# Three first column tiles on half 0, four modulation dots on VectorE, and down units of 1024 columns

## The chip, the cores and the metric

One core of a Trainium2 chip runs the whole computation as one program. The metric is device microseconds per execution. TensorE multiplies (in the profile PE, and PEld for its weight loads), VectorE (DVE), ScalarE (ACT) and GpSimd (POOL) work on tiles in SBUF or PSUM, SyncE (SP) issues the transfers. Each engine runs its own instructions strictly in the order in which they were written; semaphores make one wait for another.

## The reference, cut to what matters

Two layers work on 1024 tokens of width 1024 (a context of 256 tokens feeds only the first mixer). Layer 0 mixes with a recurrent block (RG-LRU), layer 1 with a Conformer convolution; each is followed by a gated FFN with a 3x3 depthwise convolution between its two products.

```
for i in range(DEPTH):                                   # 2
    mod = s_c @ ada_w[i] + ada_b[i]                      # 6 x 1024 modulation values
    sh1, sc1, g1, sh2, sc2, g2 = split(mod, 6)
    h = h + g1 * mixer(rmsnorm(h, norm_mix[i]) * (1 + sc1) + sh1)
    xm2 = rmsnorm(h, norm_ffn[i]) * (1 + sc2) + sh2
    u = dwconv2d(xm2 @ w_up, cw, cb, rows, width)        # 1024 -> 5632 channels, 3x3 on a 16 x 64 grid
    v, g = jnp.split(u, 2, axis=-1)
    h = h + g2 * ((silu(g) * v) @ w_down)                # 2816 -> 1024
return rmsnorm(h, norm_final)

def conformer_conv(xm, ...):
    a, g = split(xm @ w1 + b1, 2)                        # 1024 -> 2 x 1024
    v = dwconv1d(a * sigmoid(g), cw, cb)                 # 31 taps
    return silu(layernorm(v)) @ w2 + b2
```

## The kernel before

All tensors lie channels on partitions, tokens along the free dimension, so a column tile is 128 output channels by 1024 tokens. Every fp32 operand is split into a high and a low part, and a product is three matmuls (high x high, high x low, low x high). A column tile has 8 k steps of 6 matmuls, two for each of the three products, one per half of the tokens: 48 matmuls of 512 columns. PSUM is four tiles P[0] to P[3], each of two banks of 512 columns (half 0 and half 1).

**An FFN** (`ffn`, lines 1050 to 1179) runs over 22 pairs p of a value tile and a gate tile. I number the 44 column tiles t0 to t43 as they come: t2p is the value tile of pair p, t2p+1 its gate. A tile's conv (`ffn_conv`) is one ScalarE instruction that starts the accumulator `cv` from PSUM and eight VectorE instructions that add the other taps from PSUM. Then follow a SiLU on ScalarE, the product on VectorE (`cv<-cv,cv`), and the split of z into zh (ScalarE) and zl (GpSimd). The tile's PSUM place is free again when its conv is over.

The place is chosen by a counter `nt`: t0 and t1 on P[0] and P[1] (`first_pair`), each later tile on `nt % 3`, so t42 is on P[0] and t43 on P[1]. P[3] belongs to the down product: from pair 3 on, `between` issues, after every second k step of a column tile, one unit of 6 matmuls that multiplies two z tiles into one bank of P[3], the banks taking turns, and VectorE adds it to the residual h (`h<-ps,mod,h`, 512 columns). The last four z tiles go through `k_outer(4, ..., (2, 3, 0, 1))`, line 1179: it accumulates eight output tiles at a time, two in each PSUM tile, going to P[2], P[3], P[0] for its first three k, and to P[1] only with the fourth. The last gate tile's conv runs in two halves of tokens (`last_gate`).

**The start of a stage.** An RMS norm of the residual needs the sum of squares of all eight tiles (`nacc`); `norm_half` sends it through a product with a constant matrix (the stat, `ps<-nacc,ones`), a ScalarE square root and a VectorE reciprocal (`rs`), and applies it to eight tiles (`xmh`, `xml`). Half 0 is normalised while the stage before still ends; `first_pair` (line 513) then runs t0 on half 0, the stat of half 1, t1 on half 0, and both tiles on half 1. It is used at the start of both FFNs and of the Conformer.

**The modulation** of layer 1, and the last part of layer 0's, is computed during the first FFN as 56 dots of one row of `ada_w` with the vector `sC`: the row is loaded into one of two `raw` buffers, GpSimd multiplies, ScalarE sums. The `raw` buffers also take the down weights. 24 earlier dots (for layer 0's mixer) run as one VectorE instruction each.

**Order.** The kernel simulates itself while it is built (`Order`, lines 65 to 164): each operation has an assumed duration, an engine and a priority; TensorE's program is taken in the order written, and after each piece the operations of the other engines that could have started by then are emitted, the earliest start first, then the lower `prio`, then the one written first. So the written order of TensorE's work, and the assumed times, set where an instruction stands in each engine's queue. On the chip nothing overtakes.

Of the kernel before, what the change touches and what calls it, by code (L numbers as in the profile page):

```python
# [21 lines left out]
ND = D // P  # L22
# [258 lines left out]
class Net:  # L281
# [228 lines left out]
        self.act(512, hi, t, AF.Identity, [tB] + ABs, [hB], bias=B)  # L510
        self.stt(512, lo, t, B, hi.bitcast(F32), ADD, SUB, [tB, hB] + ABs, [lB])

    def first_pair(self):

        slots = [self.w_next() for _ in range(2)]
        x = lambda h, k: [(self.xmh[h][:, k, :], self.xml[h][:, k, :])]
        step = lambda i, h, k: self.k_step(
            slots[i], k, [self.P[i][:, h, :]], x(h, k), k == 0, k == ND - 1, list(self.xB[h][k]), [self.PB[i][h]])
        for i in range(2):
            for k in range(ND):  # L520
                step(i, 0, k)
            if i == 0:
                self.norm_half(*self.pending)
        for k in range(ND):
            for i in range(2):
                step(i, 1, k)

    def ada_dot(self, l, q, eng="dve", after=()):  # L530

        t, b = self.load_raw(self.a["ada"][l, q], after=after)
        col, mB = self.mod[l][:, q:q + 1], self.modB[l][q // 8]
        if eng == "dve":
            self.stt(1024, t, t, 1.0, self.sC, MULT, MULT, [b, self.sCB], [b], [mB], accum=col, after=after)
        else:
            self.tten(1024, t, t, self.sC, MULT, [b, self.sCB], [b], eng=eng)
            self.act(1024, t, t, AF.Copy, [b], [b], [mB], accum=col)

    def ada_bias(self, l, part):  # L540
        m = self.mod[l][:, part * 8:part * 8 + 8]
        b = self.modB[l][part]
        self.tten(8, m, m, self.v("ada_b", l * 48 + part * 8, 8), ADD, [b, self.vB], [b])

    def ada_scale(self, n, l, part, norm):

# [503 lines left out]
    def ffn(self, l, end, last=None):  # L1050
        o = self.o
        g2 = self.modcol(l, 5)
        dn, zr, cv = Ring(self.dn), Ring(self.zt), Ring(self.cv)
        Z, nb = {}, [0]

        def load_down(g, c0, cols, slot):

            t, b = self.raw.next()
            n = 2 * cols
            src = self.a["down"][l, 2 * g:2 * g + 2, :, c0:c0 + cols].rearrange("t p c -> p t c")  # L1060
            self.dma(t[:, :n].rearrange("p (t c) -> p t c", t=2), src, P * n * 4, w=[b])
            hi, lo, hB, lB = slot
            self.split(t[:, :n], b, (hi[:, :n], lo[:, :n], hB, lB), n=n)
            v = lambda x: x[:, :n].rearrange("p (t c) -> p t c", t=2)
            return v(hi), v(lo), hB, lB, c0

        def unit(g, d, hf, w):
            hi, lo, hB, lB, c0 = w
            b = nb[0] % 2
            nb[0] += 1  # L1070
            out, outB = self.P[3][:, b, :], self.PB[3][b]
            c, x = slice(d * P - c0, d * P + P - c0), slice(hf * 512, hf * 512 + 512)
            seq, r = [], [hB, lB]
            for i in range(2):
                zh, zl, zB = Z[2 * g + i]
                r += zB[hf]
                seq += [(hi[:, i, c], zh[:, x]), (hi[:, i, c], zl[:, x]), (lo[:, i, c], zh[:, x])]

            def go():
                for i, (w_, y) in enumerate(seq):  # L1080
                    self.mm(out, w_, y, i == 0, i == 5)

            o.pe(6 * self.mm_us, go, r, [outB])
            h, hB_ = self.h[:, d, x], self.hB[d][hf]
            self.stt(512, h, out, g2(d), h, MULT, ADD, [outB, hB_, self.modB[l][5]], [hB_], prio=-1)


        todo = []
        state = {"q": None, "n": 0, "step": 0}
        quarters = {}  # L1090

        def quarter(g, q):
            quarters[g, q] = load_down(g, q * 256, 256, dn.next())

        def between():
            state["step"] += 1
            if state["step"] % 2 == 0 and todo:
                g, q, d, hf = todo.pop(0)
                unit(g, d, hf, quarters[g, q])
                if (d, hf) == (2 * q + 1, 1):  # L1100
                    del quarters[g, q]
                    nxt = (g, q + 3) if q < 1 else (g + 1, q - 1)
                    if nxt[0] < NF // 2 - 2:
                        quarter(*nxt)

        def zsplit(p, a, aB):
            zh, zl, zhB, zlB = zr.next()
            Z[p] = zh, zl, [[zhB, zlB]] * 2
            self.act(1024, zh, a, AF.Copy, [aB], [zhB])
            self.tten(1024, zl, a, zh.bitcast(F32), SUB, [aB, zhB], [zlB], eng="pool")  # L1110

        def last_gate(f, pt, a, aB, acc, accB):

            zh, zl, zhB, zlB = zr.next()
            Z[NF - 1] = zh, zl, [[Buf(after=[b]) for b in (zhB, zlB)] for _ in range(2)]
            for h in range(2):
                b, c = Buf(after=[aB, accB]), slice(h * 512, h * 512 + 512)
                (hB, lB), av, gv = Z[NF - 1][2][h], a[:, c], acc[:, c]
                self.ffn_conv(l, f, pt, acc, b, h * 8, h * 8 + 8, -2)
                self.act(512, gv, gv, AF.Silu, [b], [b])  # L1120
                self.tten(512, av, av, gv, MULT, [b], [b], prio=-3)
                self.act(512, zh[:, c], av, AF.Copy, [b], [hB])
                self.tten(512, zl[:, c], av, zh[:, c].bitcast(F32), SUB, [b, hB], [lB], prio=-3)

        nt = 0
        ada = [(0, q) for q in range(40, 48)] + [(1, q) for q in range(48)] if l == 0 else []
        if ada:
            self.modB[0][5].begin()
            for p in range(6):
                self.modB[1][p].begin()  # L1130
        for q in range(3):
            quarter(0, q)
        for p in range(NF):
            if p >= 3 and p % 2 == 1 and p < NF - 1:
                g = (p - 3) // 2
                todo += [(g, q, d, hf) for q in range(4) for d in (2 * q, 2 * q + 1) for hf in range(2)]
            pts, accs = [], []
            if p == 0:
                self.first_pair()
                pts, nt = [0, 1], 2  # L1140
            for i, f in enumerate((p, NF + p)):
                if p:
                    self.col_tile(self.w_next(), nt % 3, between)
                    pts.append(nt % 3)
                    nt += 1
                acc, accB = cv.next()
                accs.append((acc, accB))
                if f < 2 * NF - 1:
                    self.ffn_conv(l, f, pts[i], acc, accB)
            (a, aB), (gt, gB) = accs  # L1150
            if p < NF - 1:
                self.act(1024, gt, gt, AF.Silu, [gB], [gB])
                self.tten(1024, a, a, gt, MULT, [aB, gB], [aB])
                zsplit(p, a, aB)
            else:
                last_gate(2 * NF - 1, pts[1], a, aB, gt, gB)
            for _ in range(4 if p < 3 else 3):
                if ada and p >= 1:
                    self.ada_dot(*ada.pop(0), "pool")
            if l == 0 and p == 2:  # L1160
                self.ada_bias(0, 5)

        if l == 0:
            for p in range(6):
                self.ada_bias(1, p)
            self.ada_scale(2, 1, 1, "norm_mix")
            self.ada_scale(3, 1, 4, "norm_ffn")
            m = self.mod[1][:, 16:24]
# [24 lines left out]
    def conformer(self, pool):  # L1193
# [31 lines left out]
        def summed(m):  # L1225

            for h in range(2):
# [2 lines left out]
                if m == 0:  # L1230
                    self.act(512, la, c, AF.Copy, [cvB[m][h]], [lB_])
                elif m not in LATE:
                    self.tten(512, la, la, c, ADD, [lB_, cvB[m][h]], [lB_], eng="pool")

        def taps(m, pt):

# [60 lines left out]

        for m in range(ND):
            if m == 0:
                self.first_pair()  # L1300
                sigmoid(m, 0)
            else:
                self.col_tile(self.w_next(), 0)
                sigmoid(m, 0)
                self.col_tile(self.w_next(), 1)
            glu(m, 1)
            hm = self.h[:, m, :]
# [126 lines left out]
```

## Time and profile before

| | us |
|---|---|
| median of 3 runs | 2446.95 (2445.36 to 2448.15) |
| the profiled execution | 2447.42 |
| its span, first to last instruction | 2445.6 |
| TensorE busy | 2336.1 (96%), 10440 matmuls |
| VectorE busy | 1915.0 (78%) |
| ScalarE busy | 966.6 (40%) |
| GpSimd busy | 808.0 (33%) |
| mean granted TensorE clock | 0.980 |

Busy shares are means over stages of different character. The granted clock is the share of TensorE's full speed in a stretch; 1.00 is 2.4 GHz and 0.50 is 1.2 GHz. In a timeline, the bracket at the end of a row gives how long the engine had been idle just before and which instruction's end released it. Equal instructions in a row are put together (x2, x17), with the time of all.

### The profile page before, as it was taken

Reading aid. Unit: us, or ns where it says so; the run is one execution under the profiler, and the core shown is the slowest. Engines: PE = TensorE matmul, PEld = TensorE weight load, DVE = VectorE, ACT = ScalarE, POOL = GpSimd, SP = SyncE. Lnnn points to the kernel's source line nnn. Section 1 sums busy time; section 2 is a strip of 40 time slices with the busy share of each in tenths; the row PEclk is TensorE's granted clock in tenths of the full one; section 3 lists DMA queues with packets and bytes.
Section 4 is the critical chain, followed back from the end, with each engine's and each line's share of the span. In section 5 each row is a group of like instructions: output and inputs, shape, how many; then the busy total and the mean of one; then the engine's idle time right before and its main releaser. Section 6 shows DMA issues by size and latency. Waiting matters only on the chain. (4 is left out here: it accounts for less than half of the span.)

```text
span 2445.6 us, 26204 instructions
## 1 busy us (share of the span) xinstructions
PE 2336.1 (96%) x10440; PEld 1893.9 (77%) x10440; DVE 1915.0 (78%) x1888; ACT 966.6 (40%) x1145; POOL 808.0 (33%) x413
## 2 busy tenths in 40 slices
PE   7999999889899999999998999699999999999997
PEld 2788788677688888888886888577788888888886
DVE  7677878776878778777888888677888777777877
ACT  5578778544433333333225332365322221222223
POOL 1100000355545554544423243245323322332323
PEclk9999999899999999999999999899999999999998
DMA  7324325352222323222111242422111111111101
GB/s 268 113 81 147 94 78 169 103 195 99 93 97 96 103 86 104 95 90 101 65 44 35 74 126 85 138 69 91 52 48 52 32 51 52 52 51 49 44 26 70
DMA packets 82443, 214.99 MB, mean 88 GB/s; under 512 B 8528, under 2 KB 33104, under 8 KB 82192
## 3 DMA queue, kind: packets, MB, share of 16 engines
q1 hardware_dynamic: 80448, 210.68, 26.4%
q10 hardware_dynamic: 1872, 2.62, 0.3%
q8 instruction: 82, 1.34, 0.2%
q14 instruction: 41, 0.34, 0.0%
HBM read 192.10 MB, written 13.63 MB: 84 GB/s over the span
## 5 line engine op out<-in xcount | busy, mean ns | idle before, releaser
L361 DVE SCALAR_TENSOR_TENSOR cv<-ps,vec,cv 128x960 f32<-128x960 f32 (+2 forms) x720 | 860.7, 1197 | 143.7 <-ACT cv L353 128.1
L440 PE MATMUL ps<-xmh,whi 128*128 128x512 f32 x2272 | 747.0, 396 | 19.3 <-ACT xmh L353 12.3
L440 PE MATMUL ps<-xmh,wlo 128*128 128x512 f32 x2272 | 739.9, 393 | 6.9 <-POOL wlo L368 5.2
L440 PE MATMUL ps<-xml,whi 128*128 128x512 f32 x2272 | 740.5, 393 | 4.2 <-DVE xml L361 4.1
L368 POOL TENSOR_TENSOR wlo<-wraw,whi 128x1024 fp32r<-128x1024 f32 (+1 forms) x164 | 397.8, 2440 | 703.0 <-ACT whi L353 689.4
L440 PEld LDWEIGHTS ps<-xmh,whi 128*128 128x128 f32 x2272 | 429.3, 190 | 117.7 <-ACT xmh L353 15.9
L440 PEld LDWEIGHTS ps<-xml,whi 128*128 128x128 f32 x2272 | 430.7, 190 | 102.9 <-DVE xml L361 8.4
L440 PEld LDWEIGHTS ps<-xmh,wlo 128*128 128x128 f32 x2272 | 430.2, 189 | 101.0 <-POOL wlo L368 7.8
L361 DVE SCALAR_TENSOR_TENSOR h<-ps,mod,h 128x512 f32<-128x512 f32 (+1 forms) x360 | 262.6, 733 | 161.6 <-PE ps L440 161.5
L353 ACT ACTIVATE cv<-ps,vec 128x1024 f32<-128x1024 f32 (+1 forms) x90 | 105.9, 1181 | 364.0 <-PE ps L440 352.9
L353 ACT ACTIVATE whi<-wraw 128x1024 fp32r<-128x1024 f32 (+1 forms) x198 | 202.2, 1042 | 111.0 <-DMA wraw<-w_out_in 34.1
L368 POOL TENSOR_TENSOR zl<-cv,zh 128x1024 fp32r<-128x1024 f32 x42 | 101.4, 2415 | 416.1 <-ACT zh L353 416.1
L440 PE MATMUL ps<-zh,dnh 128*128 128x512 f32 x576 | 227.8, 395 | 6.3 <-DVE h L361 5.9
L440 PE MATMUL ps<-zl,dnh 128*128 128x512 f32 x576 | 224.8, 390 | 5.0 <-POOL zl L368 5.0
L440 PE MATMUL ps<-zh,dnl 128*128 128x512 f32 x576 | 227.0, 394 | 0.0
L368 POOL TENSOR_TENSOR raw<-raw,sC 128x1024 f32<-128x1024 f32 x56 | 134.9, 2412 | 141.5 <-DMA raw<-ada_in 141.5
L353 ACT ACTIVATE cv<-cv 128x1024 f32<-128x1024 f32 (+1 forms) x46 | 47.1, 1023 | 309.3 <-DVE cv L361 301.0
L361 DVE SCALAR_TENSOR_TENSOR CV<-ps,vec,CV 128x1009 f32<-128x1009 f32 (+14 forms) x120 | 153.0, 1275 | 8.7 <-ACT CV L353 5.1
L368 POOL TENSOR_TENSOR dnl<-raw,dnh 128x512 fp32r<-128x512 f32 x72 | 93.5, 1299 | 176.6 <-ACT dnh L353 176.5
L353 ACT ACTIVATE raw<-raw 128x1024 f32<-128x1024 f32 x56 | 59.2, 1057 | 231.2 <-POOL raw L368 231.2
L440 PEld LDWEIGHTS ps<-zl,dnh 128*128 128x128 f32 x576 | 108.7, 189 | 31.2 <-POOL zl L368 5.8
L440 PEld LDWEIGHTS ps<-zh,dnh 128*128 128x128 f32 x576 | 108.4, 188 | 29.3 <-DVE h L361 6.4
(140 smaller groups left out, 2420.9 us busy)
## 6 DMA issues: line engine op xcount, KB each, us to landing
raw<-ada_in SPq DMA_DIRECT2D x88, 512.0 KB, 3.6
wraw<-up_in SPq DMA_DIRECT2D x88, 512.0 KB, 3.5
raw<-down_in SPq DMA_DIRECT2D x72, 256.0 KB, 3.1
wraw<-w_in SPq DMA_DIRECT2D x32, 512.0 KB, 3.4
wraw<-w_in_in SPq DMA_DIRECT2D x20, 512.0 KB, 3.4
wraw<-w_out_in SPq DMA_DIRECT2D x20, 512.0 KB, 3.6
wraw<-cw_in SPq DMA_DIRECT2D x16, 512.0 KB, 3.9
wraw<-gw_in SPq DMA_DIRECT2D x10, 512.0 KB, 3.9
```

Source lines behind the costliest of these rows:

```text
L353: "act", 0.2 + n * 0.00075, lambda: self.nc.scalar.activation(out, in_, func, **kw),
L361: lambda: self.nc.vector.scalar_tensor_tensor(out=out, in0=in0, scalar=scalar, in1=in1, op0=op0, op1=op1, **kw),
L368: return self.o.op(eng, dur, lambda: e.tensor_tensor(out=out, in0=in0, in1=in1, op=op), r, w, wp, prio=prio)
L440: self.nc.tensor.matmul(out, w, x, start=start, stop=stop)
```

## The change

Four things are edited.

1. `first_pair` becomes `first_tiles((0, 1, 3))`. Three column tiles start on half 0: t0, t1, then the stat of half 1, then the third tile t2 on P[3]; then t0 and t1 on half 1, then t2 on half 1. In an FFN t2 is the value tile of pair 1; in the Conformer it is the gate tile of its second pair. `nt` still starts at 2, so the FFN's t3 takes P[2].
2. The dots: four in pair 0 on VectorE, two each in pairs 1 and 2, and three a pair after that, on GpSimd, all with prio 3. The first down weights are loaded in pairs 1 and 2 and not ahead of pair 0. `ada_bias` has prio -3.
3. A down unit now covers both halves: 12 matmuls into both banks of P[3] after every fourth k step, and one instruction on VectorE that adds 1024 columns to h.
4. In the Conformer the sum of the first conv outputs on GpSimd has prio 2.

```diff
@@ first_pair -> first_tiles
-    def first_pair(self):
-        slots = [self.w_next() for _ in range(2)]
+    def first_tiles(self, pts):
+        slots = [self.w_next(n) for n in (2, 1, 1)]
...
-        for i in range(2):
+        for i in range(3):
             for k in range(ND):
                 step(i, 0, k)
-            if i == 0:
+            if i == 1:
                 self.norm_half(*self.pending)
         for k in range(ND):
             for i in range(2):
                 step(i, 1, k)
+        self.w_split(self.wq_use + 2)
+        self.w_load(self.wq_split + 2)
+        for k in range(ND):
+            step(2, 1, k)
@@ ffn: the unit
-        def unit(g, d, hf, w):
+        def unit(g, d, w):
...
             def go():
                 for i, (w_, y) in enumerate(seq):
-                    self.mm(out, w_, y, i == 0, i == 5)
-            o.pe(6 * self.mm_us, go, r, [outB])
+                    for h in range(2):
+                        self.mm(self.P[3][:, h, :], w_, y[:, h * 512:h * 512 + 512], i == 0, i == 5)
+            o.pe(12 * self.mm_us, go, r, self.PB[3])
...
-            self.stt(512, h, out, g2(d), h, MULT, ADD, [outB, hB_, self.modB[l][5]], [hB_], prio=-1)
+            self.stt(1024, h, self.P[3].rearrange("p a b -> p (a b)"), g2(d), h, MULT, ADD, [*self.PB[3], *hB_, self.modB[l][5]], hB_, prio=-1)
@@ ffn: between
-            if state["step"] % 2 == 0 and todo:
+            if state["step"] % 4 == 0 and todo:
@@ ffn: pairs
-        for q in range(3):
-            quarter(0, q)
         for p in range(NF):
...
+            if ada and p < 3:
+                for _ in range(2 if p else 4):
+                    self.ada_dot(*ada.pop(0), "pool" if p else "dve", prio=3)
+                if p == 2:
+                    self.ada_bias(0, 5)
+            for q in ((), (0,), (1, 2))[p] if p < 3 else ():
+                quarter(0, q)
             if p == 0:
-                self.first_pair()
+                self.first_tiles((0, 1, 3))
                 pts, nt = [0, 1], 2
+            if p == 1:
+                pts = [3]
             for i, f in enumerate((p, NF + p)):
-                if p:
+                if p > 1 or p and i:
                     self.col_tile(self.w_next(), nt % 3, between)
                     pts.append(nt % 3)
                     nt += 1
...
-            for _ in range(4 if p < 3 else 3):
-                if ada and p >= 1:
-                    self.ada_dot(*ada.pop(0), "pool")
-            if l == 0 and p == 2:
-                self.ada_bias(0, 5)
+            for _ in range(3 if p > 2 else 0):
+                if ada:
+                    self.ada_dot(*ada.pop(0), "pool", prio=3)
@@ conformer
-                self.first_pair()
+                self.first_tiles((0, 1, 3))
                 sigmoid(m, 0)
             else:
-                self.col_tile(self.w_next(), 0)
-                sigmoid(m, 0)
+                if m == 1:
+                    sigmoid(m, 3)
+                else:
+                    self.col_tile(self.w_next(), 0)
+                    sigmoid(m, 0)
                 self.col_tile(self.w_next(), 1)
```

The first place in the order is the start of the first FFN on TensorE. ps_65 to ps_68 are P[0] to P[3]; xmh_72 and xml_74 are half 0 of the normalised input, xmh_73 half 1; nacc_90 is the sum of squares of half 1. Before:

```order
L440 MATMUL ps_65<-xmh_72,wlo_85 128x512
L440 MATMUL ps_68<-nacc_90,ones 128x512 [waits DVE_49]
L440 MATMUL ps_66<-xmh_72,whi_86 128x512 [waits Activation_49]
...
L440 MATMUL ps_66<-xmh_72,wlo_87 128x512
L440 MATMUL ps_65<-xmh_73,whi_84 128x512 [waits Activation_49]
```

Now:

```order
L440 MATMUL ps_65<-xmh_72,wlo_85 128x512
L440 MATMUL ps_66<-xmh_72,whi_86 128x512 [waits DVE_49,Activation_49]
...
L440 MATMUL ps_66<-xmh_72,wlo_87 128x512
L440 MATMUL ps_68<-nacc_90,ones 128x512 [waits DVE_49]
L440 MATMUL ps_68<-xmh_72,whi_80 128x512 [waits Activation_49]
...
L440 MATMUL ps_68<-xmh_72,wlo_81 128x512
L440 MATMUL ps_65<-xmh_73,whi_84 128x512 [waits Activation_49]
```

The 24 matmuls of t1 on half 0 moved ahead of the stat, and the 24 of t2 stand between the stat and half 1.

The second place is the same start on VectorE. raw_76 and raw_77 are the two buffers for the dots' rows, h<-ps_68 the last flush of the stage before, A_95 the norm's scale. Before:

```order
L361 SCALAR_TENSOR_TENSOR h<-ps_68,mod_92,h 128x512 [waits PE_49]
L368 TENSOR_TENSOR nacc_90<-nacc_90,tt 128x512 [waits DVE_49,Activation_49] x2
L383 RECIPROCAL rs<-rs 128x512 [waits Activation_49]
L361 SCALAR_TENSOR_TENSOR tt<-h,A_95,rs 128x512 [waits DVE_49]
L361 SCALAR_TENSOR_TENSOR xml_75<-tt,mod_92,xmh_73 128x512 [waits Activation_49] x2
```

Now:

```order
L361 SCALAR_TENSOR_TENSOR h<-ps_68,mod_92,h 128x512 [waits PE_49]
L368 TENSOR_TENSOR nacc_90<-nacc_90,tt 128x512 [waits DVE_49,Activation_49] x2
L361 SCALAR_TENSOR_TENSOR raw_76,mod_92<-raw_76,sC 128x1024 [waits DMAHW0_49]
L361 SCALAR_TENSOR_TENSOR raw_77,mod_92<-raw_77,sC 128x1024 [waits DMAHW1_49]
L361 SCALAR_TENSOR_TENSOR raw_76,mod_92<-raw_76,sC 128x1024 [waits DMAHW3_49]
L361 SCALAR_TENSOR_TENSOR raw_77,mod_92<-raw_77,sC 128x1024 [waits DMAHW4_49]
L383 RECIPROCAL rs<-rs 128x512 [waits Activation_49]
```

The four dots stand between the last sum of squares and the reciprocal.

The third place is the end of the first FFN on TensorE: the last matmul of t43, and the first matmul into each PSUM tile of `k_outer`. whi_82 and wlo_83 are t43's weights, zh_3474 the first of the last four z tiles. Before:

```order
L440 MATMUL ps_66<-xmh_73,wlo_83 128x512
L440 MATMUL ps_67<-zh_3474,whi_84 128x512 [waits DVE_49,Activation_49]
...
L440 MATMUL ps_68<-zh_3474,whi_84 128x512
...
L440 MATMUL ps_65<-zh_3474,whi_84 128x512 [waits DVE_49,Activation_49]
...
L440 MATMUL ps_66<-zh_3474,whi_84 128x512 [waits DVE_49]
```

Now:

```order
L440 MATMUL ps_65<-xmh_73,wlo_83 128x512
L440 MATMUL ps_67<-zh_3474,whi_84 128x512 [waits DVE_49,Activation_49]
...
L440 MATMUL ps_68<-zh_3474,whi_84 128x512
...
L440 MATMUL ps_65<-zh_3474,whi_84 128x512 [waits DVE_49,Activation_49]
...
L440 MATMUL ps_66<-zh_3474,whi_84 128x512
```

t43 moved from P[1] to P[0], and `k_outer` goes to its PSUM tiles in the same order as before.

## Rows read from the trace of the kernel before

**Rows 1.** Page, part 1: busy time, share of the span, instructions.
```profile
PE 2336.1 (96%) x10440; PEld 1893.9 (77%) x10440; DVE 1915.0 (78%) x1888; ACT 966.6 (40%) x1145; POOL 808.0 (33%) x413
```

**Rows 2.** Windows: length, busy time (count) by engine, granted clock, DMA share, GB/s.
```profile
800.00:850.00 50.00, 50.00 (x220) 41.02 (x219) 38.62 (x39) 15.47 (x20) 28.20 (x14) 1.00 0.29 95
644.36:648.00 3.64, 3.64 (x10) 2.90 (x11) 3.53 (x4) 2.34 (x3) 3.64 (x2) 0.57 0.44 178
659.36:664.62 5.26, 5.26 (x13) 4.12 (x13) 2.30 (x3) 0.55 (x2) 0.00 (x0) 0.50 0.00 0
```

**Rows 3.** Timeline, TensorE, first FFN's start: start, length, instruction, [idle <-releaser].
```profile
573.73 1.02 PE L440 MATMUL ps<-nacc,ones 128*128 128x512 f32 x2
580.46 0.50 PE L440 MATMUL ps<-xmh,whi 128*128 128x512 f32 x1 [0.22 <-ACT xmh L353]
644.36 0.80 PE L440 MATMUL ps<-zl,dnh 128*128 128x512 f32 x1 [2.96 <-POOL zl L368]
659.36 0.79 PE L440 MATMUL ps<-zh,dnh 128*128 128x512 f32 x1 [5.93 <-DVE h L361]
```

**Rows 4.** Timeline, VectorE, first FFN's start.
```profile
575.51 3.35 DVE L383 RECIPROCAL rs<-rs 128x512 f32<-128x512 f32 x1 [4.82 <-ACT rs L353]
593.50 21.09 DVE L361 SCALAR_TENSOR_TENSOR cv<-ps,vec,cv 128x960 f32<-128x960 f32 x17 [2.95 <-ACT cv L353]
636.97 2.79 DVE L368 TENSOR_TENSOR cv<-cv,cv 128x1024 f32<-128x1024 f32 x1
```

**Rows 5.** Groups by line and shape, VectorE: busy us, mean ns, idle before.
```profile
L361 DVE SCALAR_TENSOR_TENSOR raw<-raw,sC 128x1024 f32<-128x1024 f32 x24 | 29.7, 1263 | 4.0 <-DMA raw<-ada_in 4.0
L361 DVE SCALAR_TENSOR_TENSOR h<-ps,mod,h 128x512 f32<-128x512 f32 x344 | 255.6, 745 | 159.2 <-PE ps L440 159.0
```

**Rows 6.** Timeline, GpSimd, same stretch.
```profile
573.09 4.73 POOL L368 TENSOR_TENSOR wlo<-wraw,whi 128x1024 fp32r<-128x1024 f32 x2
```

**Rows 7.** Timeline, TensorE and VectorE, Conformer.
```profile
1326.87 2.08 PE L440 MATMUL ps<-nacc,ones 128*128 128x512 f32 x2 [6.50 <-DVE nacc L368]
1334.86 0.40 PE L440 MATMUL ps<-xmh,whi 128*128 128x512 f32 x1
1406.94 0.73 PE L440 MATMUL ps<-xmh,wlo 128*128 128x512 f32 x2 [1.24 <-POOL wlo L368]
1506.38 1.29 DVE L361 SCALAR_TENSOR_TENSOR ps<-ps,vec,raw 128x1024 f32<-128x1024 f32 x1 [7.71 <-PE ps L440]
```

**Rows 8.** Timeline, TensorE and VectorE, second FFN's start.
```profile
1696.69 1.02 PE L440 MATMUL ps<-nacc,ones 128*128 128x512 f32 x2
1705.76 0.80 PE L440 MATMUL ps<-xmh,whi 128*128 128x512 f32 x1 [2.57 <-ACT xmh L353]
1770.45 0.78 PE L440 MATMUL ps<-zl,dnh 128*128 128x512 f32 x1 [2.06 <-POOL zl L368]
1721.12 21.09 DVE L361 SCALAR_TENSOR_TENSOR cv<-ps,vec,cv 128x960 f32<-128x960 f32 x17 [5.26 <-ACT cv L353]
1764.58 1.23 DVE L368 TENSOR_TENSOR cv<-cv,cv 128x1024 f32<-128x1024 f32 x1
```

**Rows 9.** Timeline, ScalarE, second FFN's start.
```profile
1698.29 1.28 ACT L353 ACT_TABLE_LOAD   x1
```

**Rows 10.** Timeline, TensorE and VectorE, first FFN's end.
```profile
1268.75 0.39 PE L440 MATMUL ps<-zh,whi 128*128 128x512 f32 x1
1279.90 0.50 PE L440 MATMUL ps<-zl,whi 128*128 128x512 f32 x1 [0.87 <-DVE zl L368]
1269.85 7.38 DVE L361 SCALAR_TENSOR_TENSOR cv<-ps,vec,cv 128x448 f32<-128x448 f32 x10
1279.77 2.94 DVE L361 SCALAR_TENSOR_TENSOR cv<-ps,vec,cv 128x504 f32<-128x504 f32 x4
```

**Rows 11.** Timeline, TensorE and VectorE, second FFN's end.
```profile
2386.39 0.39 PE L440 MATMUL ps<-zh,whi 128*128 128x512 f32 x1
2395.80 2.94 DVE L361 SCALAR_TENSOR_TENSOR cv<-ps,vec,cv 128x504 f32<-128x504 f32 x4
```

More of the change, by code (lines that the diff above doesn't have):

```diff
@@ L511, in apply_tile @@
         self.stt(512, lo, t, B, hi.bitcast(F32), ADD, SUB, [tB, hB] + ABs, [lB])
-    def first_pair(self):
-        slots = [self.w_next() for _ in range(2)]
+    def first_tiles(self, pts):
+        slots = [self.w_next(n) for n in (2, 1, 1)]
         x = lambda h, k: [(self.xmh[h][:, k, :], self.xml[h][:, k, :])]
         step = lambda i, h, k: self.k_step(
-            slots[i], k, [self.P[i][:, h, :]], x(h, k), k == 0, k == ND - 1, list(self.xB[h][k]), [self.PB[i][h]])
-        for i in range(2):
+            slots[i], k, [self.P[pts[i]][:, h, :]], x(h, k), k == 0, k == ND - 1, list(self.xB[h][k]), [self.PB[pts[i]][h]])
+        for i in range(3):
             for k in range(ND):
                 step(i, 0, k)
-            if i == 0:
+            if i == 1:
                 self.norm_half(*self.pending)
@@ L526, in first_pair, with ada_dot @@
                 step(i, 1, k)
-    def ada_dot(self, l, q, eng="dve", after=()):
+        self.w_split(self.wq_use + 2)
+        self.w_load(self.wq_split + 2)
+        for k in range(ND):
+            step(2, 1, k)
+    def ada_dot(self, l, q, eng="dve", after=(), prio=0):
         t, b = self.load_raw(self.a["ada"][l, q], after=after)
@@ L534, in ada_dot @@
         if eng == "dve":
-            self.stt(1024, t, t, 1.0, self.sC, MULT, MULT, [b, self.sCB], [b], [mB], accum=col, after=after)
+            self.stt(1024, t, t, 1.0, self.sC, MULT, MULT, [b, self.sCB], [b], [mB], accum=col, after=after, prio=prio)
         else:
-            self.tten(1024, t, t, self.sC, MULT, [b, self.sCB], [b], eng=eng)
+            self.tten(1024, t, t, self.sC, MULT, [b, self.sCB], [b], eng=eng, prio=prio)
             self.act(1024, t, t, AF.Copy, [b], [b], [mB], accum=col)
@@ L542, in ada_bias @@
         b = self.modB[l][part]
-        self.tten(8, m, m, self.v("ada_b", l * 48 + part * 8, 8), ADD, [b, self.vB], [b])
+        self.tten(8, m, m, self.v("ada_b", l * 48 + part * 8, 8), ADD, [b, self.vB], [b], prio=-3)
     def ada_scale(self, n, l, part, norm):
@@ L1053, in ffn @@
         dn, zr, cv = Ring(self.dn), Ring(self.zt), Ring(self.cv)
-        Z, nb = {}, [0]
+        Z = {}
         def load_down(g, c0, cols, slot):
@@ L1065, in load_down @@
             return v(hi), v(lo), hB, lB, c0
-        def unit(g, d, hf, w):
+        def unit(g, d, w):
             hi, lo, hB, lB, c0 = w
[L1069 to L1072, printed above, removed]
+            c = slice(d * P - c0, d * P + P - c0)
             seq, r = [], [hB, lB]
@@ L1075, in unit @@
                 zh, zl, zB = Z[2 * g + i]
-                r += zB[hf]
-                seq += [(hi[:, i, c], zh[:, x]), (hi[:, i, c], zl[:, x]), (lo[:, i, c], zh[:, x])]
+                r += zB[0] + zB[1]
+                seq += [(hi[:, i, c], zh), (hi[:, i, c], zl), (lo[:, i, c], zh)]
             def go():
                 for i, (w_, y) in enumerate(seq):
-                    self.mm(out, w_, y, i == 0, i == 5)
-            o.pe(6 * self.mm_us, go, r, [outB])
-            h, hB_ = self.h[:, d, x], self.hB[d][hf]
-            self.stt(512, h, out, g2(d), h, MULT, ADD, [outB, hB_, self.modB[l][5]], [hB_], prio=-1)
+                    for h in range(2):
+                        self.mm(self.P[3][:, h, :], w_, y[:, h * 512:h * 512 + 512], i == 0, i == 5)
+            o.pe(12 * self.mm_us, go, r, self.PB[3])
+            h, hB_ = self.h[:, d, :], self.hB[d]
+            self.stt(1024, h, self.P[3].rearrange("p a b -> p (a b)"), g2(d), h, MULT, ADD, [*self.PB[3], *hB_, self.modB[l][5]], hB_, prio=-1)
         todo = []
@@ L1096, in between @@
             state["step"] += 1
-            if state["step"] % 2 == 0 and todo:
-                g, q, d, hf = todo.pop(0)
-                unit(g, d, hf, quarters[g, q])
-                if (d, hf) == (2 * q + 1, 1):
+            if state["step"] % 4 == 0 and todo:
+                g, q, d = todo.pop(0)
+                unit(g, d, quarters[g, q])
+                if d == 2 * q + 1:
                     del quarters[g, q]
@@ L1135, in ffn @@
                 g = (p - 3) // 2
-                todo += [(g, q, d, hf) for q in range(4) for d in (2 * q, 2 * q + 1) for hf in range(2)]
+                todo += [(g, q, d) for q in range(4) for d in (2 * q, 2 * q + 1)]
             pts, accs = [], []
+            if ada and p < 3:
[5 more added lines that the diff above has]
+                quarter(0, q)
             if p == 0:
-                self.first_pair()
+                self.first_tiles((0, 1, 3))
                 pts, nt = [0, 1], 2
+            if p == 1:
+                pts = [3]
             for i, f in enumerate((p, NF + p)):
-                if p:
+                if p > 1 or p and i:
                     self.col_tile(self.w_next(), nt % 3, between)
@@ L1232, in summed @@
                 elif m not in LATE:
-                    self.tten(512, la, la, c, ADD, [lB_, cvB[m][h]], [lB_], eng="pool")
+                    self.tten(512, la, la, c, ADD, [lB_, cvB[m][h]], [lB_], eng="pool", prio=2)
         def taps(m, pt):
```

## The prediction

> **What bounds the kernel now.** I read the page's busy times first. TensorE is busy 96% of the span, VectorE 78% [rows 1]. The windows then show whether that 96% is even: from 800 to 850 us TensorE has no idle time at full clock, 220 products in 50 us, 0.2273 us each [rows 2], with VectorE busy 38.6 us. A saving on another engine is worth nothing there. So I went to the timelines of the places where TensorE does wait: the starts of the first FFN, the Conformer and the second FFN, and the two FFN ends. A long wait costs twice: behind the 5.93 us one, 13 products ran in 5.26 us at a granted clock of 0.50 (1.2 of 2.4 GHz), against 13 x 0.2273 = 2.96 at full clock [rows 2, 3]. That is 2.3 us more; with the first products of the wait itself I take 2.5 us for every wait of about 6 us or longer. After 1.24 us of idle the next pair took 0.73 us and no slow stretch followed [rows 7].
>
> In what follows t0, t1, ... are an FFN's column tiles in order, P0 to P3 the four PSUM tiles, "stat" the two-piece product with nacc. Times are made against the profiled 2447.42 us, 0.47 above the median.
>
> **First FFN's start.** The third tile's 24 half-0 products stand behind the stat as t1's did, so the stat moves 24 x 0.2273 = 5.45 us later, to 579.18, and the second half's first product still finds its operand: it came 6.73 us after the stat, with 0.22 us of wait [rows 3]. t0 and t1 are complete 5.45 us later, and VectorE's first conv starts at 593.50 + 5.45 = 598.95 [rows 4]. TensorE has lost nothing, since t2 is by then half done. From that conv's start to the end of t3's is 636.97 - 593.50 = 43.5 us of VectorE's own work [rows 4], so t3's PSUM tile comes free at 642.4. t6, which takes it, is wanted at 635.0 (580.46 + 5.45 + 72 x 0.2273 = 602.3 for the first three tiles, then three more of 10.9). A wait of some 7 us and the cold clock: t6 goes on as from 644.9. Before, t6 began at 636.97 and then lost 2.96 to zl, 1.4 to the clock after it (10 products in 3.64 us, not 2.27 [rows 2]), 5.93 to the flush of h and 2.5 to the clock [rows 3], so that it went on as from 650. In the new order the first flush stands before the last of t4's convs, not behind all of t5's, and units come every 24 products, so those two waits go. Gain 5 us; 0 if something takes their place, 8 if the half-clock part is not paid.
>
> **Four dots on VectorE.** 4 x 1.26 = 5.1 us [rows 5], put where VectorE was idle 4.82 us before the reciprocal [rows 4], which now comes 5.45 us later: they fit with about 5 us to spare. Cost 0; without that cover 5 us. GpSimd's two wlo splits (4.73 us) run in the same stretch [rows 6], and no row shows a dot beside one. The nearest is VectorE's product at 636.97, which took 2.79 us where the same one took 1.23 at 1764.58 [rows 4, 8]: 1.56 us more each would make the dots 11.3 us long, 1 us beyond the cover. The Trainium skill ("SBUF — State Buffer", section "SBUF: two separate sides") has a rule for this: a VectorE instruction with two SBUF inputs and a GpSimd one that reads SBUF exclude each other for the whole instruction. By that rule the dots could be late by that 1 us, and the sum below would be 2464.5. I keep 0, since two splits can delay two dots, not four.
>
> **Conformer's start.** Here the stat waited 6.50 us for nacc [rows 7]. Now t1's half 0 (5.45 us) stands ahead of it and fills that; 1.05 us of wait stay, too short for the clock by the 1.24 us row. The second half's first product came at 1334.86, 8.0 us after the stat [rows 7] since the stat itself was slow; at 6.7, as in the first FFN, it comes 1.3 us earlier, with 24 products more done: 1.3 + 5.45 = 6.7 us. VectorE's taps also start 1.3 us earlier, and it waited 7.71 us for TensorE at 1506 [rows 7], so it doesn't eat the gain. Bounds 3 (nacc later, or the taps behind) and 8.
>
> **Second FFN's start.** There the chain from the stat was late because a table load ran at 1698.29, after the stat [rows 8, 9]; with the stat 5.45 us later (1702.14) it is done before, and the operand comes 6.73 us after the stat, at 1708.9, not 9.07 after. t0 and t1 then end as early as before, 1719.8, VectorE starts at 1721.1 as before and frees t3's tile at 1764.6 [rows 8]; t6 is wanted at 1719.8 + 5.45 + 3 x 10.9 = 1758.0. It waits 6.6 and pays 2.5: as from 1767.1. Before it was 1764.58 + 2.06 for zl [rows 8] + 1.4 of clock = 1768.0. Gain 1 us, from -3 (table load still in the way) to 4.
>
> **Down units.** The same 576 products per layer go to both halves of P3. One flush of 1024 instead of two of 512 frees VectorE a little (two take 2 x 0.745 us [rows 5]; a 1024 form is not in the trace, the nearest with two inputs takes 1.26), which bounds nothing in the steady state. But P3 has no second buffer now: the next unit comes 24 products = 5.45 us after, and the flush must be done by then. VectorE waited 159 us for these 344 flushes [rows 5], so it was mostly early. I take -1 us (fewer changes between tile and unit); bounds -3 and +10.
>
> **The two FFN ends.** This is the largest term, and no line of the diff names it. With t2 on P3, every later tile sits one place back in the rotation: t42 and t43 sit on P2 and P0, where they sat on P0 and P1. The last four z's still go into P2, P3, P0 first and P1 last. So the first units now want, after 12 products, the very P0 that the last gate's conv still reads; the order shows TensorE waiting for VectorE there. That conv runs in halves from 1269.85 and is over at 1279.77 + 2.94 = 1282.7; TensorE came to P0 at 1268.75 [rows 10]. In the second FFN the conv is over at 2398.7, and TensorE came at 2386.39 [rows 11]. That is 13.95 and 12.3 us; a wait on P2 for t42's conv falls inside. Nothing else is in TensorE's order that could run meanwhile. Each pays 2.5 us of clock, and the 0.87 us wait for zl [rows 10] goes. Loss 13.95 + 12.3 + 5 - 0.87 = 30.4 us. Bounds: 24 (P0's first half free two instructions early, and 1.7 us less of clock at each end) and 34 (1.8 us more of clock at each). In the order one wait covers both halves of P0: none stands before the second half's product. The Trainium skill ("PSUM — Partial Sum Buffer", section "PSUM bank collisions raise a hardware error") asks for guards by bank. By that rule P0's first bank could go two conv instructions of 0.74 us earlier, and the sum below would be 2460.5; I go by the order.
>
> **Sum.** -5 + 0 - 6.7 - 1 - 1 + 30.4 = +16.7. The small reorderings elsewhere (mod's bias earlier in the mixer's end, prio 3 on dots) I set to 0 within 2. 2447.4 + 16.7 = 2464, less 0.5 to the median: 2463.5 us.
>
> **Rivals.**
> (a) The ends cost nothing: the last gate's conv is over when TensorE comes to P0. Then only the gains stand: 2447 - 13.7 = 2433, faster. It decides from the point where both ends together lose under 13.7 us. For it: before, one wait of 0.87 us is all that this conv caused at the first end. Against: VectorE's last conv cannot begin before t43's products end, and 12.9 us of it [rows 10] against 2.8 us of cover leaves 10 us even at once. Chance 0.06.
> (b) The single-buffered units stall again and again: with 72 units a layer, 0.3 us each is 43 us: 2463 + 43 = 2506. For it: conv instructions of 1.2 us stand ahead of a flush. Against: the idle time before flushes. Chance 0.06.
> (c) The starts give nothing, as VectorE, 5.45 us later at the first and no earlier at the others, sets the pace: 2447 + 30.4 - 1 = 2476. For it: t6 waits on VectorE in both FFNs. Against: the flush and zl waits go in any case. Chance 0.13.
> My forecast has the remaining 0.75, with its own range 2455 to 2471.
>
> **Chances.** 0.2% of the time, 4.9 us, is about what can be told from no change. Slower: forecast, (b) and (c) nearly whole, 0.90. Same: ends at half of the loss with all gains, 0.05. Faster: (a), 0.05. The range takes in (c) and leaves out (a) and (b): 2453 to 2475.
>
> **What would show it.** Right: one wait of TensorE of about 10 us on VectorE behind 12 products into P2 and P3 at each FFN end, with the clock at 0.50 after; no 5.93 us wait for h and no 6.5 us wait for nacc; a new wait of 6 us at t6. Wrong: those ends without a wait, or many short waits for the flush between 700 and 1250 us.

## The result, and the profile after

The changed kernel takes 2465.02 us (median of 4 runs, 2462.91 to 2469.16), the kernel before 2447.55 (4 runs, 2445.36 to 2449.49): a ratio of 1.0077, 95% interval 1.0062 to 1.0092, slower by 17.5 us. The forecast was 2463.5 us. The profiled execution took 2469.16 us, 4.1 above its median, with a span of 2467.3.

First the page, the line that answers to [rows 1]:

```profile
PE 2338.4 (95%) x10440; PEld 1896.2 (77%) x10440; DVE 1906.5 (77%) x1752; ACT 967.7 (39%) x1137; POOL 797.1 (32%) x409
```

TensorE has the same 10440 products and the same busy time within 2.3 us; the span is 21.7 us longer. So the difference is nearly all idle time. The waits of TensorE by what ended them (us in total, times, longest) say whose:

```profile
PE ps L440 <- DVE cv L361: 37.3, 6, 11.6
PE ps L440 <- DVE nacc L368: 5.3, 2, 4.2
PE ps L440 <- DVE h L361: 2.8, 4, 1.5
```

and before:

```profile
PE ps L440 <- DVE nacc L368: 10.7, 2, 6.5
PE ps L440 <- DVE h L361: 8.4, 3, 5.9
PE ps L440 <- DVE cv L361: 0.6, 2, 0.3
```

Waits for a conv's last read of PSUM were 0.6 us before and are 37.3 us now. Waits for nacc and for the flush of h went from 10.7 and 8.4 us to 5.3 and 2.8.

Where along the run? The stat products are marks that both traces have. TensorE's timeline, after:

```profile
583.80 1.02 PE L440 MATMUL ps<-nacc,ones 128*128 128x512 f32 x2
1307.09 1.02 PE L440 MATMUL ps<-nacc,ones 128*128 128x512 f32 x2
1710.48 1.02 PE L440 MATMUL ps<-nacc,ones 128*128 128x512 f32 x2
2432.07 1.07 PE L440 MATMUL ps<-nacc,ones 128*128 128x512 f32 x2
```

and before, the two marks that were not shown:

```profile
1294.46 1.02 PE L440 MATMUL ps<-nacc,ones 128*128 128x512 f32 x2
2410.23 1.02 PE L440 MATMUL ps<-nacc,ones 128*128 128x512 f32 x2
```

The first and third mark stand one tile of half 0 later in the new program (5.45 us), which is taken off here, and so in the kernels of the experiments that start with three tiles:

| stretch | before | after | difference | forecast |
|---|---|---|---|---|
| start to the first FFN's stat | 573.73 | 578.35 | +4.6 | 0 |
| first FFN, its end included, to the Conformer's first stat | 720.73 | 728.74 | +8.0 | +10.1 |
| Conformer, to the second FFN's stat | 402.23 | 397.94 | -4.3 | -6.7 |
| second FFN, its end included, to the last norm's stat | 713.54 | 727.04 | +13.5 | +13.3 |

(The forecast's 30.4 us for the ends are 15.6 and 14.8 here, its unit term half in each FFN.) The 4.6 us ahead of the first FFN I put down to this execution: in the profiles of the seven experiments below the same mark lies between 572.7 and 577.7, and not clearly by program. The program of the kernel before gives 572.7 (e2) and 576.1 (e3) there, that of the change 573.4 to 577.7 (e4, e6, e1, e7). Without them the change is +17.2 in the trace, +17.5 in the medians and +16.7 in the forecast's sum.

The FFNs can be split further by following the n-th of the 10440 products in both traces. In the first FFN the lag of the changed kernel goes from 4.6 us at its stat to -0.8 when the steady state begins, -1.7 just before the end and 12.6 at the Conformer's first stat: start -5.4, steady state -0.9, end +14.3. In the second it goes from 8.4 to 7.8, 6.9 and 21.8: -0.6, -0.9 and +15.0.

**The ends.** First FFN, TensorE and then VectorE, to be read against [rows 10]:

```profile
1266.05 0.47 PE L440 MATMUL ps<-zh,whi 128*128 128x512 f32 x1 [1.63 <-DVE cv L361]
1268.69 0.39 PE L440 MATMUL ps<-zh,wlo 128*128 128x512 f32 x1
1280.68 0.77 PE L440 MATMUL ps<-zh,whi 128*128 128x512 f32 x1 [11.60 <-DVE cv L361]
1267.67 7.38 DVE L361 SCALAR_TENSOR_TENSOR cv<-ps,vec,cv 128x448 f32<-128x448 f32 x10
1277.60 2.94 DVE L361 SCALAR_TENSOR_TENSOR cv<-ps,vec,cv 128x504 f32<-128x504 f32 x4
```

Twelve products go into P2 and P3, the last of them at 1268.69; then 11.60 us nothing, until the last gate's conv is over (1277.60 + 2.94 = 1280.5). Second FFN, against [rows 11]:

```profile
2391.91 0.47 PE L440 MATMUL ps<-zh,whi 128*128 128x512 f32 x1 [1.29 <-DVE cv L361]
2405.75 0.77 PE L440 MATMUL ps<-zh,whi 128*128 128x512 f32 x1 [10.80 <-DVE cv L361]
2402.67 2.94 DVE L361 SCALAR_TENSOR_TENSOR cv<-ps,vec,cv 128x504 f32<-128x504 f32 x4
```

Here the wait is 10.80 us, behind one of 1.29 for t42's conv on P2. Behind the first of the two the clock is at half for seven products, behind the second for ten:

```profile
1280.68:1283.80 3.12, 3.12 (x7) 2.45 (x8) 1.38 (x2) 1.15 (x2) 0.00 (x0) 0.50 0.00 0
2405.75:2411.00 5.25, 5.25 (x14) 4.15 (x15) 1.39 (x2) 1.15 (x2) 0.00 (x0) 0.58 0.00 0
```

Seven products took 3.12 us (1.59 at full clock), and 14 took 5.25 (3.18): 1.5 and 2.1 us for the clock.

**The starts.** TensorE at the first FFN's start [rows 3], and VectorE with GpSimd [rows 4, 6]:

```profile
586.30 0.50 PE L440 MATMUL ps<-xmh,whi 128*128 128x512 f32 x1 [0.78 <-ACT rs L353]
648.09 1.19 PE L440 MATMUL ps<-xmh,whi 128*128 128x512 f32 x2 [6.28 <-DVE cv L361]
575.24 1.22 DVE L361 SCALAR_TENSOR_TENSOR raw<-raw,sC 128x1024 f32<-128x1024 f32 x1
576.38 3.42 DVE L361 SCALAR_TENSOR_TENSOR raw<-raw,sC 128x1024 f32<-128x1024 f32 x1
579.82 3.31 DVE L361 SCALAR_TENSOR_TENSOR raw<-raw,sC 128x1024 f32<-128x1024 f32 x1
583.51 1.23 DVE L361 SCALAR_TENSOR_TENSOR raw<-raw,sC 128x1024 f32<-128x1024 f32 x1 [0.38 <-DMA raw<-ada_in]
586.28 3.35 DVE L383 RECIPROCAL rs<-rs 128x512 f32<-128x512 f32 x1 [1.53 <-ACT rs L353]
575.62 6.42 POOL L368 TENSOR_TENSOR wlo<-wraw,whi 128x1024 fp32r<-128x1024 f32 x2 [6.45 <-ACT whi L353]
```

t6 waits 6.28 us for t3's conv; the waits for zl and for the flush are gone. The four dots took 1.22, 3.42, 3.31 and 1.23 us, the two long ones beside GpSimd's two weight splits, which took 6.42 us instead of 4.73. They end at 584.7 and the reciprocal starts at 586.28, 2.48 us after the stat; before it was 1.78. A new small wait of 0.78 us is for the square root, which reads the stat's half of P3 while t2 wants the other half; it comes at all three starts.

The Conformer [rows 7]:

```profile
1339.56 1.13 PE L440 MATMUL ps<-nacc,ones 128*128 128x512 f32 x2 [1.12 <-DVE nacc L368]
1342.16 0.50 PE L440 MATMUL ps<-xmh,whi 128*128 128x512 f32 x1 [0.78 <-ACT rs L353]
1513.41 1.29 DVE L361 SCALAR_TENSOR_TENSOR ps<-ps,vec,raw 128x1024 f32<-128x1024 f32 x1 [6.45 <-PE ps L440]
1581.08 1.22 PE L440 MATMUL ps<-CV,ones 128*128 128x512 f32 x1 [10.59 <-ACT CV L353]
```

The wait for nacc is 1.12 us, not 6.50. At VectorE's wait for TensorE at 1513.41 the lag to before is 7.0 us, 5.6 less than at the stage's first mark (12.6). Of these 5.6 the Conformer's end gives back 1.3: there TensorE waited 10.59 us for CV, before 9.34. (That wait varies: in e7, whose Conformer has the same program, it was 8.27.)

The second FFN's start [rows 8, 9], ScalarE and TensorE:

```profile
1705.83 1.28 ACT L353 ACT_TABLE_LOAD   x1
1712.25 0.69 ACT L353 ACTIVATE rs<-ps,eps 128x512 f32<-128x512 f32 x1 [5.13 <-PE ps L440]
1774.11 1.19 PE L440 MATMUL ps<-xmh,whi 128*128 128x512 f32 x2 [5.65 <-DVE cv L361]
```

The table load ran ahead of the stat (1710.48), as forecast, and t6 waited 5.65 us for t3's conv.

**The steady state and the units.** A window with the new units (540 us), and VectorE's flushes:

```profile
720.00:1260.00 540.00, 540.00 (x2366) 443.63 (x2365) 414.83 (x346) 173.62 (x218) 259.97 (x124) 1.00 0.27 89
L361 DVE SCALAR_TENSOR_TENSOR h<-ps,mod,h 128x1024 f32<-128x1024 f32 x144 | 183.8, 1277 | 8.2 <-PE ps L440 8.2
```

No wait at all in 540 us, 2366 products: 0.2282 us each by this count, and over 800 to 1240 us 1928 products against 1924 before. P3 without a second buffer costs nothing; the flush of 1024 took 1277 ns.

### The profile page after: what moved, and what is told of

It reads as the page before. It is cut to its first block, busy times and chain, and to the rows that moved or that the text cites. A ratio compares the mean times of both kernels' runs of the same rounds, so it can differ in the third digit from the quotient of the medians.

```text
span 2467.3 us, 26127 instructions
## 1 busy us (share of the span) xinstructions
PE 2338.4 (95%) x10440; PEld 1896.2 (77%) x10440; DVE 1906.5 (77%) x1752; ACT 967.7 (39%) x1137; POOL 797.1 (32%) x409
## 4 chain that ended last, share of the span: by engine, by line
PE 69%; DVE 16%; ACT 7%; DMA 3%; issue 3%; POOL 1%; SPq 0%; DVEq 0%; ACTq 0%; POOLq 0%
PE ps L440 69%; DVE cv L361 4%; DVE CV L361 3%; ACT F L353 2%; DVE tt L361 1%; ACT L353 1%; ACT whi L353 1%; DVE rs L383 1%; ACT tt L353 1%; DVE F L361 1%; DVE F L761 1%; DVE F L368 1%; DMA wraw<-gw_in 1%; DVE nacc L368 1%; DVE xml L361 1%
## 5 line engine op out<-in xcount | busy, mean ns | idle before, releaser
L361 DVE SCALAR_TENSOR_TENSOR h<-ps,mod,h 128x1024 f32<-128x1024 f32 (+2 forms) x216 | 232.1, 1080 | 65.0 <-PE ps L440 65.0
L440 PE MATMUL ps<-zh,dnl 128*128 128x512 f32 x576 | 179.4, 392 | 0.0
L440 PE MATMUL ps<-zl,dnh 128*128 128x512 f32 x576 | 179.1, 392 | 0.0
L440 PE MATMUL ps<-zh,dnh 128*128 128x512 f32 x576 | 178.1, 390 | 0.0
L368 POOL TENSOR_TENSOR raw<-raw,sC 128x1024 f32<-128x1024 f32 x52 | 125.2, 2409 | 152.2 <-DMA raw<-ada_in 152.2
L353 ACT ACTIVATE cv<-cv 128x1024 f32<-128x1024 f32 (+1 forms) x46 | 47.1, 1024 | 302.2 <-DVE cv L361 302.0
L440 PEld LDWEIGHTS ps<-zh,dnl 128*128 128x128 f32 x576 | 108.2, 188 | 24.2
```

What stands on the lines that cost most here:

```text
L353: "act", 0.2 + n * 0.00075, lambda: self.nc.scalar.activation(out, in_, func, **kw),
L361: lambda: self.nc.vector.scalar_tensor_tensor(out=out, in0=in0, scalar=scalar, in1=in1, op0=op0, op1=op1, **kw),
L368: return self.o.op(eng, dur, lambda: e.tensor_tensor(out=out, in0=in0, in1=in1, op=op), r, w, wp, prio=prio)
L440: self.nc.tensor.matmul(out, w, x, start=start, stop=stop)
```

## The experiments

Each median is compared with the kernel before, run beside it on the same chip; ratios have 95% intervals.

| kernel | median us | ratio to before |
|---|---|---|
| the change | 2465.02 | 1.0077 (1.0062 to 1.0092) |
| e1, the change with the old rotation at the ends | 2434.11 | 0.9954 (0.9941 to 0.9968) |
| e2, before with only the conflict at the ends | 2475.62 | 1.0120 (1.0106 to 1.0133) |
| e3, before with only the new units | 2439.44 | 0.9972 (0.9961 to 0.9982) |
| e4, two tiles in the FFNs, three in the Conformer | 2425.20 | 0.9912 (0.9899 to 0.9926) |
| e5, e4 with the old dots | 2424.33 | 0.9908 (0.9893 to 0.9923) |
| e6, e4 with two tiles in the Conformer | 2427.94 | 0.9919 (0.9905 to 0.9932) |
| e7, the change with the old dots | 2467.45 | 1.0078 (1.0064 to 1.0092) |

**e1, the change with t42 and t43 back on P0 and P1.**

```diff
-                self.first_tiles((0, 1, 3))
-                pts, nt = [0, 1], 2
+                self.first_tiles((1, 2, 3))
+                pts, nt = [1, 2], 3
```

> The changed kernel, with one thing different: in the FFNs the first three tiles go to P1, P2 and P3 and t3 to P0, so that the last pair t42, t43 sits on P0 and P1 again, and the down product's order (P2, P3, P0, then P1) meets a free P0. Theory (the rotation's wait at the two FFN ends cost 14.2 + 14.8 us, and the starts gained): about 29 us less than the changed kernel, 2436 us, 11 faster than the kernel before, with no wait over 2 us at 1265 to 1300 and at 2385 to 2415. Rival (the ends wait because VectorE is late there after the change, wherever the tile sits): within 5 us of the changed kernel's 2465.

Measured 2434.11 us. Two lines of the program are different, and 31 us are gone. TensorE's timeline has t6's wait as in the changed kernel, and at the first end only a wait for zl; the second end has none:

```profile
644.81 1.19 PE L440 MATMUL ps<-xmh,whi 128*128 128x512 f32 x2 [6.23 <-DVE cv L361]
1274.15 0.51 PE L440 MATMUL ps<-zl,whi 128*128 128x512 f32 x1 [0.50 <-DVE zl L368]
```

By the marks, the first FFN takes 713.6 us against 728.7 in the changed kernel, the second 711.2 against 727.0: 15.2 and 15.8 us, nearly all of it at the two ends. So the rotation is the cause, and all else in the change together is 11 to 12 us faster than before.

**e2, the kernel before with the same conflict put in.**

```diff
-        order = [pts, (0, 2, 1, 3) if pts[0] else pts]
+        order = [pts, (1, 2, 0, 3) if pts[0] else pts]
...
-        self.k_outer(4, zsrc, flush, lambda bank: end(bank), (2, 3, 0, 1), last=last)
+        self.k_outer(4, zsrc, flush, lambda bank: end(bank), (2, 3, 1, 0), last=last)
```

> The kernel before, with the places of P0 and P1 in the down product's last stage exchanged (P2, P3, P1, P0, and P1, P2, P0, P3 for the second half), so that the third PSUM tile asked for is the one that the last gate's conv reads. Nothing else differs. Theory: the ends alone cost 26 to 30 us, so 2474 to 2478 us, with one wait of 10 to 12 us at each end. Rival (the loss needs the new down units or the later starts): under 10 us, 2447 to 2457.

Measured 2475.62, 29.6 us above the kernel before that ran beside it (2445.97). The two waits:

```profile
1281.68 0.77 PE L440 MATMUL ps<-zh,whi 128*128 128x512 f32 x1 [13.92 <-DVE cv L361]
2411.35 0.77 PE L440 MATMUL ps<-zh,whi 128*128 128x512 f32 x1 [12.33 <-DVE cv L361]
```

13.92 and 12.33 us: what [rows 10, 11] gave (13.95 and 12.3), since here VectorE has the same lead as before. The ends cost this without any other part of the change.

**e3, the kernel before with only the units over both halves** (`unit`, `between` and `todo` of the change, nothing else).

```diff
-            if state["step"] % 2 == 0 and todo:
+            if state["step"] % 4 == 0 and todo:
...
-            o.pe(6 * self.mm_us, go, r, [outB])
+            o.pe(12 * self.mm_us, go, r, self.PB[3])
```

> The kernel before with only the down units of both halves (12 products into both banks of P3 after every fourth k step, one flush of 1024). Theory: the waits for zl (2.96 us) and for the flush of h (5.93 us) at the first FFN's start go, since a unit starts later in t6 and a flush has longer: 5 to 10 us faster, 2437 to 2442. Rival 1 (a single buffer in P3 makes each unit wait for the flush): 0.3 us for each of 144 units, 2490. Rival 2 (these waits only turn into a wait for t7's or t8's PSUM tile): within 3 us of 2447.

Measured 2439.44: 6.5 us faster, inside the first range, but not quite for its reason. The wait for zl went, at both starts; the wait for the flush did not:

```profile
662.01 1.22 PE L440 MATMUL ps<-zh,dnh 128*128 128x512 f32 x2 [8.79 <-DVE h L361]
```

It grew from 5.93 to 8.79 us, as the first flush still stood behind all of t5's conv in VectorE's order. By the marks the FFNs are 4.0 and 4.75 us shorter. Followed by product, 3.1 and 3.9 us of that are gained at the starts, where the zl wait goes with its clock (2.96 + 1.4 us in the first FFN, partly used up by the longer wait for the flush, and 2.06 + 1.4 in the second), and 0.9 us in each steady state, where 3 to 4 more products fit into 440 us.

**e4, three tiles only in the Conformer.**

```diff
             if p == 0:
-                self.first_tiles((0, 1, 3))
+                self.first_pair()
                 pts, nt = [0, 1], 2
-            if p == 1:
-                pts = [3]
             for i, f in enumerate((p, NF + p)):
-                if p > 1 or p and i:
+                if p:
```

> The changed kernel with the FFNs starting with two tiles again (t0, stat, t1, then half 1; tiles on P0, P1, P2 in turn as in the kernel before), three tiles only in the Conformer; dots and units as in the change. Theory (VectorE's convs bound the FFN starts, and a third tile ahead of half 1 makes them start 5.45 us later in the first FFN): no wait at the ends; the first FFN's t6 waits 0 to 1 us, not 6.3, so 5 to 8 us less than the e1 kernel's time, the second FFN gains 0 to 3: about 2429 us. Rival (three tiles gain in the FFN starts as well, since half 1's operand is late there too): 2436 or more, not faster than e1.

Measured 2425.20, the fastest of all but for e5, and 9 us below e1, which differs in the FFN starts alone. From 600 to 700 us the only wait of TensorE is

```profile
629.92 0.70 PE L440 MATMUL ps<-xmh,whi 128*128 128x512 f32 x2 [0.29 <-DVE cv L361]
```

where e1 waited 6.23 us for t3's conv. So a third tile ahead of half 1 is a loss at an FFN's start: VectorE has four tiles' convs to do before t6 can go on, and the third tile moves their start back. By the marks 3.9 us in the first FFN, 5.1 in the second.

**e5, e4 with the dots of the kernel before.**

```diff
-            if ada and p < 3:
-                for _ in range(2 if p else 4):
-                    self.ada_dot(*ada.pop(0), "pool" if p else "dve", prio=3)
...
+            for _ in range(4 if p < 3 else 3):
+                if ada and p >= 1:
+                    self.ada_dot(*ada.pop(0), "pool")
```

> The e4 kernel (FFNs start with two tiles, Conformer with three, new units) with the dots where the kernel before had them: none on VectorE in pair 0, four on GpSimd in each of pairs 1 and 2. Theory: in e4 the four dots stood between nacc and the first conv, two of them among the norm's tiles, where GpSimd's work held them up, and TensorE waited 1.66 + 0.46 us for xml; that goes: about 2 us less, 2423. Rival (the four dots a pair on GpSimd delay zl and the weights' low parts, as the 2.96 us wait of the kernel before): a wait for zl at 640 to 655, 2426 to 2430.

Measured 2424.33, ratio 0.9908 against e4's 0.9912: no difference that can be told; by the marks the first FFN, where the dots run, takes 709.8 us against 709.7. Each expectation was half right. In e4 TensorE's longest wait at the start was for xml, among whose tiles the planner had put two of the dots; in e5 that is gone and a wait for the first flush, not for zl, stands later. TensorE in e4, and then in e5:

```profile
591.10 0.50 PE L440 MATMUL ps<-xml,whi 128*128 128x512 f32 x1 [1.66 <-POOL xml L368]
```

```profile
655.31 1.22 PE L440 MATMUL ps<-zh,dnh 128*128 128x512 f32 x2 [2.71 <-DVE h L361]
```

**e6, e4 with two tiles in the Conformer as well.**

```diff
-                self.first_tiles((0, 1, 3))
+                self.first_pair()
                 sigmoid(m, 0)
             else:
-                if m == 1:
-                    sigmoid(m, 3)
-                else:
-                    self.col_tile(self.w_next(), 0)
-                    sigmoid(m, 0)
+                self.col_tile(self.w_next(), 0)
+                sigmoid(m, 0)
```

> The e4 kernel with the Conformer's start of the kernel before as well (two tiles, the stat after the first). It shows what the third tile is worth in the Conformer alone. Theory (the prediction's 6.7 us; the trace of the changed kernel shows 4.3 left at the Conformer's end, as ScalarE's wait for CV there grew by 1.25): 4 to 7 us more than e4, 2429 to 2432, with a wait for nacc of 6.5 us and the clock low behind it. Rival (the Conformer is bound by VectorE's taps, and the gain is eaten at its end): within 1.5 us of e4's 2425.

Measured 2427.94, ratio 0.9919: 2.7 us above e4 by medians, less than expected, and the intervals overlap. The wait for nacc is back, with TensorE's slow stat behind it:

```profile
1315.81 2.08 PE L440 MATMUL ps<-nacc,ones 128*128 128x512 f32 x2 [6.51 <-DVE nacc L368]
```

By the marks the Conformer takes 402.6 us here, and 401.6, 402.2 and 400.9 in the other three profiles with two tiles (e3, before, e2), against 395.2, 395.2, 397.1, 397.8 and 397.9 with three (e4, e5, e1, e7, the change): about 3 to 7.4 us, 5.2 by the means. The medians of e4 and e6 show 2.7; their runs spread over 5.3 and 3.5 us, and e4's profile is of its fastest run, 3.8 us below its median, which flatters it. Which of the figures is nearer stays open.

**e7, the change with the dots of the kernel before** (the edit of e5, made in the changed kernel).

> The changed kernel with the dots where the kernel before had them. Theory (the dots, 9.4 us long beside GpSimd's two weight splits, end 1.5 us before the reciprocal and cost nothing): within 1.5 us of the changed kernel, 2463.5 to 2466.5. Rival 1 (they cost on VectorE): 2 to 5 us less. Rival 2 (GpSimd's dots in pairs 1 and 2 delay zl for the first units): 2 to 5 us more.

Measured 2467.45, ratio 1.0078 against 1.0077. The runs spread over 9 us, so the medians alone would not exclude the rivals' 2 us; by the marks the first FFN takes 728.0 us against 728.7 and the second 727.2 against 727.0. The dots cost and give nothing beyond these differences.

## Why the prediction was right

The time (2463.5 forecast, 2465.0 measured) came out for the reason given. That it came out within 0.5 us of the forecast's sum (+17.2 in the trace, +16.7) is in part luck: the Conformer gave 2.4 us less than forecast, and the ends (1.1), the units (0.8) and, by a little, the first start (0.4) made that up, with 0.4 lost at the second start. By steps:

- *The two ends*, the largest term, 30.4 us; 14.3 + 15.0 = 29.3 measured. e1 took 31 us out by undoing the rotation alone and e2 put 29.6 us in by adding it alone. The waits themselves were forecast well: TensorE came to P0 13.5 us (first end: t43 over at 1264.42, 12 products of 0.2333, first product at 1280.68) and 12.3 us later than unhindered, against 13.95 and 12.3. The clock was taken at 2.5 us for each and was 1.5 and 2.1.
- *One wait for both halves of P0.* The product came 0.1 us after the conv's last instruction, not two instructions sooner. So the sum by the order was right. The Trainium skill ("PSUM — Partial Sum Buffer", section "PSUM bank collisions raise a hardware error") asks for guards by bank; by that, an estimate from the conv's rows, P0's first half could have gone about 1.5 us earlier. The program guards both halves together, and no run here tried it.
- *First FFN's start*, 5 us; 5.4 measured. The step on t6 was right: 6.28 us waited, some 7 forecast. VectorE's first conv started at 605.05, that is 1.5 us later than 593.50 + 5.45 + 4.6: the square root's wait and ScalarE's order were not in the working.
- *Four dots*, 0. Right, e7. Two dots were held for 2.2 and 2.1 us. They were two and not four, as GpSimd had two instructions there, and the cover took it. The Trainium skill ("SBUF — State Buffer", section "SBUF: two separate sides") has such a pair exclude each other for the whole instruction. The trace agrees: the two dots and the two splits, 1.22 + 1.22 + 4.73 us alone, took from 575.62 to 583.13 us together.
- *Conformer*, 6.7 us, mis-sized: 5.6 at 1513 us and 4.3 at its end (5.2 in the mean over all profiles, e6). The stat went at full clock and the wait for nacc was 1.12 as forecast, but half 1's first product came 7.5 us after the stat, not 6.7, and 1.3 us were lost in the longer wait for CV.
- *Second FFN's start*, 1 us; 0.6 measured. The table load and the wait at t6 came as forecast.
- *Units*, 1 us, mis-sized: 0.9 us in the steady state of each FFN, 1.8 in all, and the zl waits are theirs too (e3), which the working had put to the starts. For the flush's wait the working gave two reasons. That units come less often was not one: in e3 that wait grew. The place of the first flush was: VectorE did seven of t4's eight convs before it in the change, all eight in e4, four of t5's too in e5 (2.71 us of wait), and all of t5's in the kernel before (5.93) and in e3 (8.79).

Rival (a) fell with e2, (b) with the empty steady state. Rival (c) fell as a sum, since the starts gave 10 us, but not in its reason: the third tile gives nothing in the FFNs. It costs about 9 us there (e1 against e4), which in the change is covered by what the units give (8.75 by the marks of e3). Its 2476 us also lies just outside the range of 2453 to 2475 that was said to take it in.

The version to keep is e4: the new units and the Conformer's third tile, FFNs started with two tiles, 0.9912 of the time before (0.9899 to 0.9926), 21 us.

## What to carry to other kernels

When an edit shifts a counter that picks buffers round robin, write down which buffer the last item gets, and who asks for it first; here 30 us hung on that and no line of the diff spoke of it. Work that fills a wait of the bounding engine also delays whatever it stands ahead of: worth it where the engine waits for data (the Conformer), a loss where the next engine in line has the longer queue (the FFNs). The two-way proof is cheap: undo the suspect in the new kernel, and put it alone into the old one.

## What the runs showed of the hardware

The half clock behind a long wait does not grow with the wait: after 11.60 us it lasted for seven products, after 10.80 us for ten, after 13.92 and 12.33 us for seven (e2), and after 5.93 us for twelve ([rows 2] count the thirteenth, which starts as that window ends); the extra time was 1.5 to 2.5 us. Nor is a short wait safe: the first end's 1.63 us for t42's conv had no slow stretch behind it, but behind e4's 1.66 us for xml, which two waits of 0.46 and 0.73 us precede, the clock was at half for eight products and took 1.6 us. e4's window:

```profile
591.60:594.60 3.00, 3.00 (x9) 2.30 (x9) 2.78 (x1) 0.73 (x1) 3.00 (x2) 0.54 0.33 132
```

The prediction's "too short for the clock", for a wait of 1.05 us, held in the Conformer. A VectorE instruction of 1.22 us with both inputs in SBUF took 3.3 to 3.4 us beside a GpSimd one of 2.4 us, and the GpSimd pair grew too, from 4.73 to 6.42 us: each engine held the other up.
